# The mean of squares of a norm is read from PSUM by ScalarE, not VectorE

## The chip, the cores and the metric

The kernel runs on one core of a Trainium2 chip. A core has a matrix engine (TensorE, PE in the profile), and beside it VectorE (DVE), ScalarE (ACT), GpSimd (POOL) and SyncE (SP, which here issues the loads and stores). They run side by side, each in its own order of instructions, and wait for each other through semaphores. TensorE writes its results into PSUM, the other engines work on SBUF and PSUM. The metric is the device time of one execution in microseconds, lower is better.

## What is computed

One decoder block on a sequence of 2048 tokens with 1024 channels in fp32. Cut to what matters here:

```python
def rmsnorm(x, g):
    r = lax.rsqrt(jnp.mean(x * x, axis=-1, keepdims=True) + EPS)
    return x * r * g

hn = rmsnorm(h, norm1_g)
u_pool, q, k, v = split(hn @ w_in)
y_pool = pool_mixer(u_pool, pool_w, pool_scale)         # 4 causal window means, each mapped 128x128
o = stick_breaking_attention(q, k, v)                   # 8 heads of 64
mixed = concat([rmsnorm(y_pool, pool_out_g), rmsnorm(o, attn_out_g)])
h = h + mixed @ w_out
up = rmsnorm(h, norm2_g) @ w_up                         # 1024 -> 4096
h = h + jnp.square(jax.nn.relu(up)) @ w_down            # 4096 -> 1024
return rmsnorm(h, final_g)
```

There are five kinds of norm: before the input projection, over the pooled half, over the attention half, before the up projection, and the final one. Each is made once for each block of 512 tokens.

## The kernel before

The 2048 tokens are four blocks of 512; a block lies as 8 chunks of 128 channels (the partitions) by 512 tokens. Products keep fp32 accuracy by splitting both operands: ScalarE makes the high part (L146, `hi`), VectorE the low part as the difference (L147), and `products` (L178 to L180) issues three matmuls for each pair of chunks. A rounded operand and its rest are written in one tile, so `hl<-raw` by ACT is the high part of a weight granule and `hl<-raw,hl` by DVE its low part; `h<-nt` and `h<-nt,h` are the same for the normed activation, `sa`, `hw`, `ad`, `wd` for the operands of the feed-forward. Weight granules are loaded five ahead (`weights`, `load_raw`).

The stages in order of time: the input projection of the four blocks (`pd` tiles) with the pooling groups (`pp`) between; attention (`pz` scores, a running product on VectorE as `pc`, `pta` transposes, `po` values), cut into small pieces that are put between the matmuls of the projection; the output projection with the residual; the up projection (`pX`, `pY`, `pZ`, L1082) and the down projection (`pb`, L1249 and L1422), both by a scheme that needs seven block products instead of eight and so has sums on VectorE (L919 to L922, L1021 to L1048).

A norm goes through the engines in a fixed chain. ScalarE and VectorE sum the squares of the chunks (`ss`). TensorE multiplies by a column of 1/n, which gives the mean of squares `pm` with the tokens on partitions, 128 x 4 (L205). VectorE reads `pm` out of PSUM, adds epsilon and writes `m` into the SBUF tile `v` (L213). GpSimd makes the root in `v`: a first guess by integer arithmetic (L214) and three Newton steps of four instructions (L221 to L224), then casts the root to its high part and takes the low part (L241 and L242 as `yr`, L821 and L822 as `yrlast` for the last block, L1290 and L1291 for the final norm). TensorE then spreads the root over 128 partitions with 8 small matmuls (L231, `pr`), the first of which needs the cast. ScalarE copies `pr` out (`r`, L251), and VectorE multiplies the chunks (`nt<-xt,gains,r`, L263). Of the 21 roots that a run makes, 18 are made by GpSimd; the first norm of all and the last two roots of the end are made on VectorE instead.

The norm before the up projection of the last block is special: its root is made in two halves of a tile `yrlast` (`root_last`), called at step 1 of the loop in `up`, and its two spreads are written at steps 6 and 10 of that loop.

No order of instructions is written down for the machine: the framework's scheduler takes the program as written, with its own estimate of how long every instruction takes, and sets one order on each engine. The instructions of `inv_rms` have a raised priority. So an instruction that moves between engines also changes the order around it. There is a second branch for inputs that need more of the attention; it is not executed.

Of the kernel before, what the change touches and what calls it, by code (L numbers as in the profile page):

```python
# [12 lines left out]
AF = mybir.ActivationFunctionType  # L13
ALU = mybir.AluOpType
# [18 lines left out]
EPS = 1e-6  # L33
# [13 lines left out]
def hymba_block(ctx: ExitStack, tc: tile.TileContext, xT, gains, w_in, pool_w, w_out, w_up, w_down, out):  # L47
    nc = tc.nc
# [160 lines left out]
    def inv_root(pm, eng):  # L209

        v, w = vp.tile([P, 3 * TB], F32, tag="v", name="v"), pm.shape[-1]
        m, y, t = v[:, 0:w], v[:, TB:TB + w], v[:, 2 * TB:2 * TB + w]
        nc.vector.tensor_scalar(m, pm, 1.0, EPS, op0=ALU.mult, op1=ALU.add)  # L213
        eng.tensor_scalar(y.bitcast(I32), m.bitcast(I32), -0.5, float(0x5F3759DF), op0=ALU.mult, op1=ALU.add)  # L214
        for _ in range(3):
            if eng is nc.vector:
                eng.scalar_tensor_tensor(t, y, -0.5, y, op0=ALU.mult, op1=ALU.mult)
                eng.tensor_tensor(t, t, m, ALU.mult)
                eng.scalar_tensor_tensor(y, t, 1.5, y, op0=ALU.add, op1=ALU.mult)
            else:  # L220
                eng.tensor_tensor(t, y, y, ALU.mult)  # L221
                eng.tensor_tensor(t, t, m, ALU.mult)
                eng.tensor_scalar(t, t, -0.5, 1.5, op0=ALU.mult, op1=ALU.add)
                eng.tensor_tensor(y, y, t, ALU.mult)  # L224
        return y
# [9 lines left out]
    def inv_rms(ss, n, r=None, eng=None, early=False):  # L235

        eng = eng or nc.gpsimd
        with tc.high_priority():
            y = inv_root(mean_squares([ss], n, psz if early else None, "pz" if early else "px"), eng)
            yr = tmp.tile([P, 2, TB], F32R, tag="yr", name="yr")  # L240
            eng.tensor_copy(yr[:, 0], y)  # L241
            eng.tensor_tensor(yr[:, 1], y, yr[:, 0].bitcast(F32), ALU.subtract)  # L242
            where, tag = (psx, "px") if eng is nc.vector else (psz, "pz") if early else (pst, "pt")
            pr = where.tile([P, T], F32, tag=tag, name="pr")
            marks["pr"] = spread(pr, yr)
            if eng is not nc.vector:
                g = state["tick"]
                gates.extend([(g + 10, marks["pm"]), (g + 14, marks["pr"])])
            if r is None:
                r = tmp.tile([P, T], F32, tag="r", name="r", bufs=2)  # L250
            nc.scalar.activation(r, pr, AF.Copy)  # L251
            return r
# [566 lines left out]
    def root_last(i, ss, where=None, tag="px"):  # L819
        y = inv_root(mean_squares([ss], D, where, tag), nc.gpsimd)  # L820
        nc.gpsimd.tensor_copy(yrlast[:, i, 0], y)  # L821
        nc.gpsimd.tensor_tensor(yrlast[:, i, 1], y, yrlast[:, i, 0].bitcast(F32), ALU.subtract)  # L822
# [275 lines left out]
    def down(pools):  # L1098
# [187 lines left out]
        def final_root(j, acc, ss, r):  # L1286

            y = inv_root(mean_squares([ss], D, psb, f"b{free}"), nc.gpsimd)
            yr = tmp_.tile([P, 2, TB], F32R, tag="yr", name="yr", bufs=3)
            nc.gpsimd.tensor_copy(yr[:, 0], y)  # L1290
            nc.gpsimd.tensor_tensor(yr[:, 1], y, yr[:, 0].bitcast(F32), ALU.subtract)  # L1291
            roots.append((j, acc, r, yr))
# [321 lines left out]
```

## Time and profile before

| what | value |
|---|---|
| median of 3 runs | 1913.86 us (1912.65 to 1914.35) |
| profiled execution, its own time | 1917.71 us |
| its span | 1915.9 us |
| granted TensorE clock, mean | 0.995 |
| TensorE busy | 1891.8 us, 99% |
| VectorE busy | 1424.4 us, 74% |
| ScalarE busy | 1006.7 us, 53% |
| GpSimd busy | 177.7 us, 9% |

The profile is one execution; its own time is 3.85 us above the median of the runs. Start times are counted from the span's start. In a timeline row stand start, length, engine, line, operation, output and inputs with their shapes, how many, and in brackets the idle time before the row with what ended it. In a waits row stand the total of the waits, how many, and the longest.

### The profile page before, as it was taken

Reading aid. Unit: us, or ns where it says so; the run is one execution under the profiler, and the core shown is the slowest. Engines: PE = TensorE matmul, PEld = TensorE weight load, DVE = VectorE, ACT = ScalarE, POOL = GpSimd, SP = SyncE. Lnnn points to the kernel's source line nnn. Section 1 sums busy time; section 2 is a strip of 40 time slices with the busy share of each in tenths; the row PEclk is TensorE's granted clock in tenths of the full one; section 3 lists DMA queues with packets and bytes.
Section 4 is the critical chain, followed back from the end, with each engine's and each line's share of the span. In section 5 each row is a group of like instructions: output and inputs, shape, how many; then the busy total and the mean of one; then the engine's idle time right before and its main releaser. Section 6 shows DMA issues by size and latency. Waiting matters only on the chain.

```text
span 1915.9 us, 26510 instructions
## 1 busy us (share of the span) xinstructions
PE 1891.8 (99%) x8995; PEld 1577.8 (82%) x8995; DVE 1424.4 (74%) x2128; ACT 1006.7 (53%) x1598; POOL 177.7 (9%) x399
## 2 busy tenths in 40 slices
PE   9999999999999999999999999999999999999997
PEld 7888888888888888788888888887888888888886
DVE  6887799667866886776787877786655547888874
ACT  5565566555554465455566555454333345656643
POOL 0211113101211030000000000000010010020120
PEclk9999999999999999999999999999999999999998
DMA  6686596787887867776777677778998889899862
GB/s 213 204 270 201 191 295 221 244 312 264 283 321 295 282 239 252 261 254 227 273 285 269 233 258 262 243 266 310 379 358 308 282 253 314 291 297 334 295 209 91
DMA packets 206034, 509.68 MB, mean 266 GB/s; under 512 B 24256, under 2 KB 30400, under 8 KB 202048
## 3 DMA queue, kind: packets, MB, share of 16 engines
q1 hardware_dynamic: 201136, 499.24, 75.1%
q0 software_dynamic: 4608, 8.39, 2.4%
q8 instruction: 73, 1.20, 0.3%
q14 instruction: 73, 0.60, 0.1%
q10 hardware_dynamic: 144, 0.26, 0.0%
HBM read 335.82 MB, written 171.97 MB: 265 GB/s over the span
## 4 chain that ended last, share of the span: by engine, by line
PE 89%; DMA 4%; DVE 4%; issue 1%; ACT 1%; POOL 0%; SPq 0%; DVEq 0%; ACTq 0%
PE pY L1082 16%; PE pb L1422 16%; PE pb L1249 12%; PE pZ L1082 8%; PE pd L178 8%; PE pd L180 8%; PE pd L179 8%; PE pX L1082 4%; PE po L675 2%; PE pta L664 1%; DMA xt<-in_xT_dram 1%; PE pr L231 1%; DMA t<-in_w_down_dram 1%; PE pm L205 1%; PE pz L617 1%; DMA wr<-in_w_down_dram 1%
## 5 line engine op out<-in xcount | busy, mean ns | idle before, releaser
L1082 PE MATMUL pY<-sa,hw 128*128 128x512 f32 x1536 | 365.7, 389 | 0.7 <-ACT u L1015 0.7
L1422 PE MATMUL pb<-ad,wd 128*128 128x512 f32 x1488 | 340.9, 390 | 1.3 <-ACT ad L146 1.2
L1082 PEld LDWEIGHTS pY<-sa,hw 128*128 128x128 f32 x1536 | 288.1, 188 | 60.9 <-ACT u L1015 1.1
L1422 PEld LDWEIGHTS pb<-ad,wd 128*128 128x128 f32 x1488 | 278.5, 188 | 60.0 <-ACT ad L146 1.6
L178 PE MATMUL pd<-h,hl 128*128 128x512 f32 x752 | 299.8, 399 | 0.7 <-DVE qkr L424 0.7
L180 PE MATMUL pd<-h,hl 128*128 128x512 f32 x752 | 296.9, 395 | 0.0
L179 PE MATMUL pd<-h,hl 128*128 128x512 f32 x752 | 296.7, 395 | 0.0
L147 DVE TENSOR_TENSOR ad<-ar,ad 128x1024 fp32r<-128x1024 f32 x148 | 179.8, 1221 | 70.2 <-ACT ad L146 70.0
L1249 PE MATMUL pb<-ad,wd 128*128 128x512 f32 x1008 | 229.2, 389 | 0.5 <-DVE ad L147 0.5
L1249 PEld LDWEIGHTS pb<-ad,wd 128*128 128x128 f32 x1008 | 189.0, 188 | 40.4 <-DVE ad L147 1.2
L146 ACT ACTIVATE ad<-ar 128x1024 fp32r<-128x1024 f32 x148 | 155.6, 1053 | 116.8 <-issue 47.6
L1082 PE MATMUL pZ<-sa,hw 128*128 128x512 f32 x768 | 186.7, 390 | 1.5 <-DVE a L1032 1.5
L1082 PEld LDWEIGHTS pZ<-sa,hw 128*128 128x128 f32 x768 | 143.9, 188 | 32.2 <-DVE a L1032 2.4
L178 PEld LDWEIGHTS pd<-h,hl 128*128 128x128 f32 x752 | 142.1, 189 | 28.2 <-DVE qkr L424 1.0
L180 PEld LDWEIGHTS pd<-h,hl 128*128 128x128 f32 x752 | 141.8, 189 | 28.0
L179 PEld LDWEIGHTS pd<-h,hl 128*128 128x128 f32 x752 | 142.0, 189 | 27.1
L146 ACT ACTIVATE hl<-raw 128x512 fp32r<-128x512 f32 x168 | 104.0, 631 | 111.2 <-PE pd L180 70.7
L147 DVE TENSOR_TENSOR hl<-raw,hl 128x512 fp32r<-128x512 f32 x168 | 114.1, 685 | 53.6 <-ACT hl L146 50.0
L147 DVE TENSOR_TENSOR hw<-rt,hw 128x512 fp32r<-128x512 f32 x128 | 86.8, 686 | 51.4 <-ACT hw L146 51.3
L1009 ACT ACTIVATE a<-a 128x512 f32<-128x512 f32 x96 | 59.5, 630 | 86.8 <-DVE a L1048 41.4
L146 ACT ACTIVATE wd<-wr 128x1024 fp32r<-128x1024 f32 x40 | 42.4, 1060 | 112.4 <-PE pb L1422 94.1
L1082 PE MATMUL pX<-sa,hw 128*128 128x512 f32 x384 | 93.1, 389 | 0.0
(219 smaller groups left out, 2652.2 us busy)
## 6 DMA issues: line engine op xcount, KB each, us to landing
ar<-sd SPq DMA_DIRECT2D x100, 512.0 KB, 5.4
wr<-in_w_down_dram SPq DMA_DIRECT2D x64, 512.0 KB, 5.4
rb<-in_w_up_dram SPq DMA_DIRECT2D x30, 1024.0 KB, 6.4
sd<-a SPq DMA_DIRECT2D x112, 256.0 KB, 4.0
raw<-in_w_in_dram SPq DMA_DIRECT2D x50, 512.0 KB, 4.5
ar<-sdi SPq DMA_DIRECT2D x48, 512.0 KB, 5.7
sd<-s SPq DMA_DIRECT2D x88, 256.0 KB, 4.0
sdi<-hr SPq DMA_DIRECT2D x72, 256.0 KB, 4.4
```

The lines of the kernel that those rows point to most:

```text
L146: nc.scalar.activation(hi, src, AF.Copy)
L147: return nc.vector.tensor_tensor(lo, src, hi.bitcast(F32), ALU.subtract)
L178: nc.tensor.matmul(ps, hl[:, 0, c], hi, start=(k == 0), stop=False)
L179: nc.tensor.matmul(ps, hl[:, 0, c], lo, start=False, stop=False)
L180: mm = nc.tensor.matmul(ps, hl[:, 1, c], hi, start=False, stop=(k == n - 1))
L205: marks["pm"] = nc.tensor.matmul(pm[:, c:c + 1], ss[:, c * P:(c + 1) * P], inv[n], start=(i == 0), stop=(i == len(parts) - 1))
L231: mm = nc.tensor.matmul(pr[:, b * P:(b + 1) * P], yr[:, x, b:b + 1].to_broadcast([P, P]), identr, start=(b == 0 and x == 0), stop=(b == TB ...
L675: nc.tensor.matmul(po[:, p * 256 + to:p * 256 + to + hi - lo], vw[:, 2 * p + v], at[:, x, lo:hi], start=(p == 0 and n == 0 and x == 0), sk ...
L1009: nc.scalar.activation(t, src, AF.Relu)
L1082: nc.tensor.matmul(t, w[:, wx, c], a[:, ax, c % 2], start=first and c == 0 and x == 0, stop=last and c == G - 1 and x == 2, skip_group_che ...
L1249: nc.tensor.matmul(b, t[:, wx, 2 * (kk % 2) + c, i * P:(i + 1) * P], a[:, ax, c], start=p in ("P1", "P5", "P2") and kk == 0 and c == 0 and ...
L1422: nc.tensor.matmul(ps[q, n], block(t, wx, c, n), left_[q][:, ax, c], start=(n_ in ("P1", "P3") and kk == 0 and c == 0 and x == 0), stop=(n ...
```

## The change

In `inv_root`, the read of `pm` goes to ScalarE where the root is made on GpSimd, as a copy with epsilon as its bias. The three roots that VectorE makes keep their read.

```diff
         v, w = vp.tile([P, 3 * TB], F32, tag="v", name="v"), pm.shape[-1]
         m, y, t = v[:, 0:w], v[:, TB:TB + w], v[:, 2 * TB:2 * TB + w]
-        nc.vector.tensor_scalar(m, pm, 1.0, EPS, op0=ALU.mult, op1=ALU.add)
+        if eng is nc.vector:
+            nc.vector.tensor_scalar(m, pm, 1.0, EPS, op0=ALU.mult, op1=ALU.add)
+        else:
+            nc.scalar.activation(m, pm, AF.Copy, bias=EPS)
         eng.tensor_scalar(y.bitcast(I32), m.bitcast(I32), -0.5, float(0x5F3759DF), op0=ALU.mult, op1=ALU.add)
```

The lines behind it stand three further down in the changed file (L1082 is L1085, L231 is L234). The number of instructions is the same but for 18 that change the engine; the scheduler sets another order. At the places below, the numbers behind names tell apart the tiles of one name.

TensorE at the up projection, before, at the two spreads of the last block's root (`pr_8313` for the first half of `yrlast`, `pr_8410` for the second):

```order
L231 MATMUL pr_8313<-identr_103,yrlast_146 128x128 x8
L1082 MATMUL pX_8353<-sa_7869,hw_8269 128x512 x2
L1082 MATMUL pY_8129<-sa_8121,hw_8144 128x512 x6
L1082 MATMUL pY_8129<-sa_8126,hw_8144 128x512 x6
...
L1082 MATMUL pZ_8397<-sa_7908,hw_8323 128x512 x6
L231 MATMUL pr_8410<-identr_103,yrlast_146 128x128 x8
L1082 MATMUL pY_8272<-sa_8121,hw_8346 128x512 x6
```

The same place after:

```order
L234 MATMUL pr_8313<-identr_103,yrlast_146 128x128 x8
L1085 MATMUL pX_8353<-sa_7869,hw_8269 128x512 x2
L234 MATMUL pr_8410<-identr_103,yrlast_146 128x128
L1085 MATMUL pY_8129<-sa_8121,hw_8144 128x512 x6
L1085 MATMUL pY_8129<-sa_8126,hw_8144 128x512 x6
...
L1085 MATMUL pZ_8397<-sa_7908,hw_8323 128x512 x6
L234 MATMUL pr_8410<-identr_103,yrlast_146 128x128 x7
```

The first of the eight matmuls of the second spread has moved ahead of 70 matmuls, to the place behind two of `pX_8353`; the other seven stay where all eight were. ScalarE's read of the mean for this second half stands right behind the high part of `sa_8154`; VectorE's order there is the same, less the read.

VectorE before, late in the input projection, with the read for the pooled half's norm (`v_5682<-pm_5677`):

```order
L147 TENSOR_TENSOR at_5512<-pta_5507,at_5512 128x512
L147 TENSOR_TENSOR hl_5640<-raw_5536,hl_5640 128x512
L213 TENSOR_SCALAR v_5682<-pm_5677 128x4
L147 TENSOR_TENSOR at_5585<-pta_5580,at_5585 128x512
L629 SCALAR_TENSOR_TENSOR pc_5612<-sh_5618 128x256 x2
```

ScalarE after, at the same place:

```order
L146 ACTIVATE at_5512<-pta_5507 128x512
L146 ACTIVATE hl_5640<-raw_5536 128x512
L216 ACTIVATE v_5682<-pm_5677 128x4
L146 ACTIVATE at_5585<-pta_5580 128x512
L626 ACTIVATE sh_5618<-pz_5611 128x512
```

The read stands behind the split of the same weight granule `hl_5640` on either engine: behind its low part before, behind its high part after. On TensorE the spread of this root, `pr_5700`, which stood behind the five score matmuls of `pz_5719` and five of `pd_5742`, stands after the change between the second and the third of those score matmuls.

TensorE in the tail, before, at the first two spreads of the final norm (`ad` and `wd` with the numbers of one step of the down projection):

```order
L1422 MATMUL pb_17161<-ad_17151,wd_17148 128x512 x6
L231 MATMUL pr_17249<-identr_103,yr_17212 128x128
L1422 MATMUL pb_17168<-ad_17151,wd_17148 128x512
L231 MATMUL pr_17249<-identr_103,yr_17212 128x128 x7
...
L1422 MATMUL pb_17168<-ad_17246,wd_17243 128x512 x6
L1422 MATMUL pb_17175<-ad_17246,wd_17243 128x512 x6
L1422 MATMUL pb_17154<-ad_17306,wd_17303 128x512
L231 MATMUL pr_17366<-identr_103,yr_17329 128x128 x8
```

After:

```order
L1425 MATMUL pb_17161<-ad_17151,wd_17148 128x512 x6
L1425 MATMUL pb_17168<-ad_17151,wd_17148 128x512 x6
L1425 MATMUL pb_17175<-ad_17151,wd_17148 128x512
L234 MATMUL pr_17249<-identr_103,yr_17212 128x128 x8
...
L1425 MATMUL pb_17168<-ad_17246,wd_17243 128x512 x6
L234 MATMUL pr_17366<-identr_103,yr_17329 128x128 x8
L1425 MATMUL pb_17175<-ad_17246,wd_17243 128x512 x6
```

The first spread comes seven matmuls later, the second seven earlier. ScalarE reads the second mean behind the high part of `ad_17423`; VectorE read it behind eight scalings of finished chunks (L1299) and ahead of the low parts of `wd_17303` and `ad_17423`.

In the first stage, the spread of the second block's first norm, `pr_858`, comes seven matmuls earlier on TensorE. Behind it, before, ten matmuls of `pd_1386` (which takes that block's chunks) were followed by the 24 of `pd_1509` (which takes the first block's) and then by the rest of `pd_1386`; after, nineteen of `pd_1386` come first. VectorE multiplies the first three chunks of that block ahead of one more low part and one more pooling sum.

## The prediction

> **What bounds the kernel now.** I read the page's busy shares first, then the chain of work that ended last, then the table of TensorE's waits.
>
> ```profile
> PE 1891.8 (99%) x8995; PEld 1577.8 (82%) x8995; DVE 1424.4 (74%) x2128; ACT 1006.7 (53%) x1598; POOL 177.7 (9%) x399
> PE 89%; DMA 4%; DVE 4%; issue 1%; ACT 1%; POOL 0%; SPq 0%; DVEq 0%; ACTq 0%
> PE pr L231 <- DVE pc L629: 2.5, 1, 2.5
> PE pZ L1082 <- DVE a L1032: 1.5, 2, 1.2
> PE pr L231 <- POOL yr L1290: 0.9, 1, 0.9
> PE pd L178 <- DVE qkr L424: 0.7, 1, 0.7
> ```
>
> TensorE is the bound: 1891.8 us busy, and 89% of the last chain. VectorE and ScalarE have spare time, so an instruction taken from one and put on the other is worth nothing by itself. What counts is whether TensorE waits somewhere. In the waits (total, times, longest) two are a norm's spread `pr`, held by the root: 2.5 us and 0.9 us (POOL's root ends last in both, as its rows below show). So I look at each norm: when the mean is read, when the root is cast, and when TensorE reaches the spread.
>
> **The moved read itself.** It leaves VectorE at 0.155 us and arrives on ScalarE at a price the trace does not show.
>
> ```profile
> L213 DVE TENSOR_SCALAR v<-pm x19: 136/155/164, 31.8 to 1864.5; 128x4 f32<-128x4 f32 x19
> L146 ACT ACTIVATE at<-pta 128x512 fp32r<-128x512 f32 x56 | 33.4, 599 | 11.6 <-PE pta L664 9.5 <-PE po L675 1.4
> L146 ACT ACTIVATE at<-pta 128x384 fp32r<-128x384 f32 x8 | 4.0, 495 | 3.7 <-PE pta L664 3.6
> ```
>
> The nearest rows are ScalarE copies out of PSUM. 512 elements take 0.599 us and 384 take 0.495, so the line through both puts 4 elements at 0.495 − 380 × 0.104/128 = 0.19 us. The lower bound is VectorE's 0.14, the upper the 0.495 of the nearest row. I take 0.19, an estimate; 18 × 0.19 = 3.4 us on an engine 53% busy, which I cost at nothing: idle ScalarE time hides it. VectorE gains 18 × 0.155 = 2.8 us it does not need. What changes the time is the new order: TensorE's spreads are placed elsewhere. I go through the places where the rows leave less than 1 us of room or the spread moved; elsewhere I book nothing.
>
> **The last-block norm (703 to 717 us), the largest term.** Start and length are the first two columns, but for the first row: a step of POOL, shortest/median/longest ns.
>
> ```profile
> L214 POOL TENSOR_SCALAR v<-v x18: 192/193/6379, 63.9 to 1864.8; 128x4 int32<-128x4 int32 x18
> 703.32 0.95 PE L205 MATMUL pm<-inv,sslast 128*128 128x1 f32 x8
> 703.95 1.05 ACT L146 ACTIVATE sa<-sr 128x1024 fp32r<-128x1024 f32 x1
> 706.37 0.15 DVE L213 TENSOR_SCALAR v<-pm 128x4 f32<-128x4 f32 x1
> 706.62 6.38 POOL L214 TENSOR_SCALAR v<-v 128x4 int32<-128x4 int32 x1 [27.09 <-DVE v L213]
> 716.76 0.19 POOL L821 CAST yrlast<-v 128x4 fp32r<-128x4 f32 x1
> 712.88 2.88 PE L1082 MATMUL pY<-sa,hw 128*128 128x512 f32 x12
> 728.75 1.00 PE L231 MATMUL pr<-identr,yrlast 128*128 128x128 f32 x8
> 705.17:712.95 7.78, 7.78 (x40) 6.58 (x39) 7.78 (x13) 5.91 (x10) 6.33 (x1) 1.00 0.64 226
> ```
>
> The last row is busy time in that stretch (length, PE, PEld, DVE, ACT, POOL, clock, DMA share, GB/s): VectorE is busy for all of it, and POOL's first step of the root, 0.193 us in its usual rows, sits there for 6.38 us. VectorE's work there is mostly operations on two SBUF tensors. POOL gets on when VectorE pauses at 713, and the cast that TensorE needs ends at 716.95. Before, that costs nothing: the spread is at 728.75. After, its first matmul stands right behind two `pX` matmuls and ahead of the twelve of `pY`, where TensorE is at 712.88. The read moves up: pm ends at 704.27, ScalarE's `sa` at 705.00, so the mean is there at about 705.2 instead of 706.52. But POOL's step then falls on the same VectorE run, whose order is unchanged but for the read. So the cast still ends at about 716.9, and TensorE stands still for 716.9 − 712.9 = 4.0 us. Bounds: 0 (the cast is ready) and 4.2.
>
> A wait also slows the clock afterwards, as the next place shows: I add 1.7 us, bounds 0 and 3.4 (two slices). **Term: +5.7.**
>
> **The stall at 457 us.**
>
> ```profile
> 447.98 1.02 PE L205 MATMUL pm<-inv,ss 128*128 128x1 f32 x8
> 452.76 0.64 ACT L146 ACTIVATE hl<-raw 128x512 fp32r<-128x512 f32 x1 [3.21 <-DMA raw<-in_w_in_dram]
> 454.03 0.15 DVE L213 TENSOR_SCALAR v<-pm 128x4 f32<-128x4 f32 x1
> 460.08 0.51 POOL L241 CAST yr<-v 128x4 fp32r<-128x4 f32 x1
> 457.73 0.39 PE L179 MATMUL pd<-h,hl 128*128 128x512 f32 x1
> 460.64 0.33 PE L231 MATMUL pr<-identr,yr 128*128 128x128 f32 x1 [2.52 <-DVE pc L629]
> 462.19:465.60 3.41, 3.41 (x10) 2.63 (x9) 2.68 (x4) 1.20 (x3) 0.00 (x0) 0.50 0.96 325
> ```
>
> The mean is ready at 449, but VectorE first makes the low part of `hl_5640`, whose load arrived at 452.7. On ScalarE the read stands behind the high part of that same `hl_5640`, so the load still holds it: it comes at 453.5, some 0.5 us earlier. The cast comes 0.2 to 0.6 earlier (VectorE's low part still holds POOL to about 454.1). Yet the spread stands six matmuls, 6 × 0.23 = 1.4 us, earlier. So the wait grows from 2.5 to about 3.5: **+1.0**, bounds +0.5 and +2.7 (a second slow slice). The windows row is the price of a gap: for 3.41 us behind it the granted clock is 0.50, which loses half of it, 1.7 us; that is paid already and stays.
>
> The Trainium skill, TensorE: Matmul & The Clock Gate, Part 1, warns of idle gaps over about 3.4 us; this trace disagrees, since 2.52 us of idling sufficed. By that rule the sum without the slow slices that I add would be 2.6 us less, 1922.
>
> **The first stage (60 to 85 us).**
>
> ```profile
> 60.53 0.62 ACT L146 ACTIVATE hl<-raw 128x512 fp32r<-128x512 f32 x1
> 63.61 0.15 DVE L213 TENSOR_SCALAR v<-pm 128x4 f32<-128x4 f32 x1
> 70.09 0.19 POOL L241 CAST yr<-v 128x4 fp32r<-128x4 f32 x1
> 71.43 0.22 PE L231 MATMUL pr<-identr,yr 128*128 128x128 f32 x1
> 72.70 0.60 ACT L251 ACTIVATE r<-pr 128x512 f32<-128x512 f32 x1 [1.79 <-PE pr L231]
> 73.38 2.07 DVE L263 SCALAR_TENSOR_TENSOR nt<-xt,gains,r 128x512 f32<-128x512 f32 x3
> 81.05 0.50 PE L178 MATMUL pd<-h,hl 128*128 128x512 f32 x1 [0.70 <-DVE qkr L424]
> ```
>
> ScalarE is free at 61.15, so the read comes 2 us earlier, but POOL's first step waits for a gap in VectorE's run near 63.6: the cast gains 0 to 0.5 us. The spread stands seven matmuls (1.6 us) earlier, so it waits about 0.2, and `r` and the normed chunks come some 1.4 us earlier. The order spends this and more: it runs nineteen matmuls of `pd_1386` in a row where before it ran ten and then the 24 of `pd_1509`, which need no new chunk. TensorE is at the fourth chunk at 80.1; VectorE, at 0.6 to 0.7 us a step from 72.0 in its new order, has that chunk's low half at 80.9 (wait 0.5), the sixth's at 82.7 (0.5), the seventh's source at 83.4, copied at 84.1 (1.2), and frees the bank of `pd_1509` by `qkr` at 85.3 (1.0). That is 0.2 + 0.5 + 0.5 + 1.2 + 1.0 = 3.4 against the 1.0 of before (0.70, and 0.27 just ahead of it): **+2.4**, bounds −1 (all of before's waits go) and +5 (the attention pieces, now packed closer behind, wait twice more for 1.3 us).
>
> **The tail (1820 to 1838 us).**
>
> ```profile
> 1820.44 0.33 PE L231 MATMUL pr<-identr,yr 128*128 128x128 f32 x1 [0.87 <-POOL yr L1290]
> 1824.21 0.95 PE L205 MATMUL pm<-inv,ss 128*128 128x1 f32 x8
> 1825.38 1.04 ACT L146 ACTIVATE ad<-ar 128x1024 fp32r<-128x1024 f32 x1
> 1827.77 0.15 DVE L213 TENSOR_SCALAR v<-pm 128x4 f32<-128x4 f32 x1
> 1828.01 2.23 POOL L214 TENSOR_SCALAR v<-v 128x4 int32<-128x4 int32 x1 [7.33 <-DVE v L213]
> 1835.53 0.19 POOL L1290 CAST yr<-v 128x4 fp32r<-128x4 f32 x1
> 1836.26 1.00 PE L231 MATMUL pr<-identr,yr 128*128 128x128 f32 x8
> ```
>
> The first spread moves seven matmuls later (1.6 us), so its 0.87 us wait goes: −0.9. The second moves seven earlier, on a TensorE that is 0.9 earlier: it is reached at 1836.26 − 0.9 − 1.6 = 1833.8. Its mean is read on ScalarE behind `ad`, at 1826.5, but VectorE's two-tensor run (the eight scaled chunks, `wd`, `ad`) still holds POOL to about 1830.5; the cast stays near 1836.0. Wait 2.2, with half a slow slice (0.9): **+2.2** for both, bounds −0.9 and +3.0.
>
> **Given back later:** TensorE's two waits at `pZ` (1.5 us) fall behind the new wait at 713, on work that VectorE and the loads do meanwhile. I take half, **−0.7**, bounds 0 and −1.5.
>
> Sum: 5.7 + 1.0 + 2.4 + 2.2 − 0.7 = +10.6 us. The profiled run took 1917.71 us (span 1915.9), 3.85 over the median of 1913.86; the sum goes onto the median: 1924.5.
>
> **The rivals.**
> *POOL gets in between VectorE's instructions.* If a waiting POOL step ran at the end of the VectorE instruction in progress, the 14 steps would need about 10 boundaries before 712.95 and 4 × 0.28 us behind: cast at 714.3, wait 1.4, no slow slice (0.87 us brought none), and no second wait in the tail. Sum 1.4 + 1.0 + 2.4 − 0.9 − 0.2 = +3.7, 1917.6. Against it speaks the 6.38 us row, where some twelve boundaries passed. The Trainium skill, SBUF — State Buffer, section on the two separate sides, says the shared port pair is locked "for the whole instruction" only, which is this rival; the trace disagrees.
> *The gains of an earlier root win (faster).* Place: the stall at 457. If the load of `hl_5640` came at 449.6 or earlier, 3.1 us before now, the mean would be read at 450.4 and the cast be there when TensorE is: 2.5 + 1.7 = −4.2, 1909.7. It decides only if the wait at 713 is under 0.4. Against it: nothing in the change moves that load.
> *The change does nothing of note.* Casts come as the new order expects, the first stage sheds its 1.0 us, and 457's +1.0 is all that is left: 1913 to 1915.
> *Each gap costs whole slow slices.* Two at 713, one more at 457 and in the tail, the first stage at +5: 4.0 + 3.4 + 2.7 + 5 + 3.0 = +18, 1932.
>
> **How the numbers follow.** Forecast 0.60 (1918.5 to 1930); POOL between instructions 0.13, half of it under the bound; nothing of note 0.07; faster 0.06; whole slices 0.14. A change of under 0.2%, 3.8 us, can't be told from none here: faster 0.06, same 0.07 + 0.06 = 0.13, slower 0.81. The range leaves out the faster rival, and the ends of the others: 1914.5 to 1932.
>
> **What would show it.** A wait of about 4 us at the single matmul of the second `yrlast` spread, with a POOL row of some 6 us ahead of it and a clock slice near 0.50 behind; 3.5 us at the 457 spread; four short waits in the 80s; no wait at the first tail spread and about 2 at the second. I am wrong if POOL's root is not held at 705, if VectorE's run there breaks up, or if ScalarE's read costs microseconds.

## The result, and the profile after

The changed kernel takes 1923.61 us (median of 7 runs, 1918.35 to 1929.42), the kernel before 1913.48 us (7 runs, 1912.15 to 1914.35). The ratio is 1.0058 with a 95% interval of 1.0042 to 1.0075: the change costs 10 us. The profiled run took 1929.42 us, its span is 1927.6 us; it is the slowest of the seven, 5.8 us above their median, so single profiles show the places of the cost better than its size. Two later measurements of the same kernel gave 1.0065 and 1.0071, so the cost is 10 to 13 us.

The busy shares and the chain of the changed kernel:

```profile
PE 1896.9 (98%) x8995; PEld 1579.8 (82%) x8995; DVE 1420.8 (74%) x2110; ACT 1009.6 (52%) x1616; POOL 180.3 (9%) x399
PE 82%; DVE 7%; DMA 7%; issue 1%; ACT 1%; POOL 1%; SPq 0%; DVEq 0%; ACTq 0%
```

VectorE lost 18 instructions and 3.6 us of busy time, ScalarE gained 18 and 2.9 us, and neither matters. The span grew by 11.7 us, TensorE's busy time by 5.1 (matmuls at half clock are longer), the rest is idling. The chain says the same: VectorE and the loads have a larger part in it. TensorE's waits, with total, times and longest:

```profile
PE pr L234 <- POOL yrlast L824: 2.6, 1, 2.6
PE pm L205 <- DVE ss L189: 2.5, 1, 2.5
PE pZ L1085 <- DVE a L1035: 1.9, 1, 1.9
PE pr L234 <- POOL yr L1293: 1.5, 1, 1.5
PE ptv L444 <- DVE vf L439: 0.9, 1, 0.9
PE pd L178 <- DVE qkr L427: 0.7, 1, 0.7
PE pd L178 <- ACT h L146: 0.6, 1, 0.6
PE pd L179 <- DVE h L147: 0.5, 1, 0.5
PE po L678 <- ACT qk L146: 0.4, 1, 0.4
```

The first row is the new wait at the second `yrlast` spread. The second is the stall that stood at 457 us: in this profile it is ahead of the mean, not behind it. The fourth is the second spread of the tail. The last five are new or lie at another place, and all in the first stage.

The moved read itself costs what a small copy out of PSUM costs (shortest, median and longest in ns):

```profile
L216 ACT ACTIVATE v<-pm x18: 153/174/206, 58.8 to 1875.9; 128x4 f32<-128x4 f32 x18
```

**Where the time is.** The table gives the time that TensorE lost in a stretch, in us: the distance from one matmul's start to the next, less the usual distance for that shape, summed. It holds the waits and the half-clock matmuls behind them. The last three columns are experiments (below); where there are several profiles of one kernel, each is given, in the order of the runs.

| us from the start | before | changed, 3 profiles | second spread put back, 2 | early read put back | last block alone, 2 |
|---|---|---|---|---|---|
| 0 to 25 | 5.9 | 3.2, 5.1, 3.0 | 3.3, 4.0 | 4.3 | 3.5, 5.3 |
| 75 to 125 | 2.4 | 8.0, 10.3, 8.0 | 6.4, 6.5 | 2.4 | 2.6, 2.4 |
| 425 to 475 | 6.1 | 5.5, 7.3, 6.4 | 5.6, 6.4 | 7.2 | 6.2, 4.2 |
| 675 to 725 | 0.1 | 5.7, 1.0, 6.9 | 0.9, 0.6 | 3.9 | 1.8, 1.8 |
| 775 to 825 | 2.1 | 2.6, 0.6, 0.2 | 0.3, 0.5 | 1.8 | 1.4, 1.1 |
| 1000 to 1050 | 0.0 | 1.0, 0.9, 0.3 | 0.6, 1.5 | 0.8 | 0.0, 0.2 |
| 1800 to 1850 | 1.3 | 3.7, 1.8, 1.8 | 1.8, 3.5 | 3.7 | 1.3, 1.3 |
| whole span | 31.8 | 43.2, 41.0, 39.3 | 31.4, 35.4 | 36.0 | 29.1, 27.8 |

The first row is the start of the kernel, which the change does not touch: it differs by 2 to 3 us from execution to execution. Three places carry the cost: the first stage, the last block's spread, and the tail.

**The first stage.** TensorE's waits in the timeline between 77 and 83 us, and where the attention pieces stand:

```profile
78.11 0.50 PE L179 MATMUL pd<-h,hl 128*128 128x512 f32 x1 [0.53 <-DVE h L147]
81.24 0.51 PE L178 MATMUL pd<-h,hl 128*128 128x512 f32 x1 [0.59 <-ACT h L146]
82.44 0.50 PE L178 MATMUL pd<-h,hl 128*128 128x512 f32 x1 [0.70 <-DVE qkr L427]
...
112.53 0.35 PE L678 MATMUL po<-at,vw 128*128 128x256 f32 x1 [0.44 <-ACT qk L146]
113.07 0.56 PE L678 MATMUL po<-at,vw 128*128 128x256 f32 x3 [0.19 <-DVE at L147]
114.57 0.66 PE L444 MATMUL ptv<-ident,vf 128*128 128x128 f32 x4 [0.94 <-DVE vf L439]
```

With a shorter one at 79.4 us, the waits around 80 us lose 2.7 us, those at the attention pieces 2.1. Behind the latter, the matmuls run at half clock for one slice, though only 1.50 us (3.41 − 1.91) of the slice ahead of it were idle. In the windows (length; busy time of PE, PEld, DVE, ACT, POOL; granted clock; DMA share; GB/s) the slice in which the pieces wait, and the next:

```profile
112.16:115.57 3.41, 1.91 (x11) 1.52 (x12) 3.38 (x7) 2.32 (x5) 0.00 (x0) 1.00 0.86 269
115.57:118.99 3.42, 3.42 (x10) 2.64 (x9) 3.42 (x8) 0.63 (x1) 1.10 (x1) 0.50 0.95 325
```

**The last block's norm.** The changed kernel at the second `yrlast` spread:

```profile
706.23 0.16 ACT L216 ACTIVATE v<-pm 128x4 f32<-128x4 f32 x1
706.47 6.79 POOL L217 TENSOR_SCALAR v<-v 128x4 int32<-128x4 int32 x1 [25.87 <-ACT v L216]
717.11 0.19 POOL L824 CAST yrlast<-v 128x4 fp32r<-128x4 f32 x1
714.11 0.67 PE L1085 MATMUL pX<-sa,hw 128*128 128x512 f32 x2
717.35 0.47 PE L234 MATMUL pr<-identr,yrlast 128*128 128x128 f32 x1 [2.56 <-POOL yrlast L824]
717.62 5.43 PE L1085 MATMUL pY<-sa,hw 128*128 128x512 f32 x12
```

The read is early, GpSimd's first step is held for 6.79 us all the same, TensorE waits 2.56 us, and the twelve `pY` matmuls behind it take 5.43 us where they took 2.88 before.

**The tail.**

```profile
1830.01 1.00 PE L234 MATMUL pr<-identr,yr 128*128 128x128 f32 x8
1834.16 0.15 ACT L216 ACTIVATE v<-pm 128x4 f32<-128x4 f32 x1
1836.56 2.84 POOL L226 TENSOR_SCALAR v<-v 128x4 f32<-128x4 f32 x1
1844.17 1.28 PE L234 MATMUL pr<-identr,yr 128*128 128x128 f32 x8 [1.50 <-POOL yr L1293]
```

The first spread no longer waits; the second waits 1.50 us, with half clock behind it. In the other two profiles of the changed kernel the second waits 1.25 us and keeps its clock.

### The profile page after: what moved, and what is told of

Read it like the earlier page. It is cut to its first block, busy times and chain, and to the rows that moved or that the text cites. A ratio compares the mean times of both kernels' runs of the same rounds, so it can differ in the third digit from the quotient of the medians.

```text
span 1927.6 us, 26508 instructions
## 1 busy us (share of the span) xinstructions
PE 1896.9 (98%) x8995; PEld 1579.8 (82%) x8995; DVE 1420.8 (74%) x2110; ACT 1009.6 (52%) x1616; POOL 180.3 (9%) x399
## 4 chain that ended last, share of the span: by engine, by line
PE 82%; DVE 7%; DMA 7%; issue 1%; ACT 1%; POOL 1%; SPq 0%; DVEq 0%; ACTq 0%
PE pb L1425 16%; PE pY L1085 14%; PE pb L1252 12%; PE pd L178 7%; PE pd L179 7%; PE pd L180 7%; PE pZ L1085 7%; PE pX L1085 3%; PE po L678 2%; DMA sr<-su 1%; PE pta L667 1%; DMA t<-in_w_down_dram 1%; PE pr L234 1%; PE pz L621 1%; PE pz L620 1%
## 5 line engine op out<-in xcount | busy, mean ns | idle before, releaser
L1085 PE MATMUL pY<-sa,hw 128*128 128x512 f32 x1536 | 368.7, 391 | 1.5 <-ACT u L1018 0.9
L1085 PEld LDWEIGHTS pY<-sa,hw 128*128 128x128 f32 x1536 | 289.4, 189 | 63.5 <-ACT u L1018 2.5
L1085 PE MATMUL pZ<-sa,hw 128*128 128x512 f32 x768 | 186.4, 389 | 1.9 <-DVE a L1035 1.9
L1085 PEld LDWEIGHTS pZ<-sa,hw 128*128 128x128 f32 x768 | 143.9, 188 | 32.3 <-DVE a L1035 2.3
L1085 PE MATMUL pX<-sa,hw 128*128 128x512 f32 x384 | 93.2, 390 | 0.0
```

The costliest lines, as they stand in the source:

```text
L1085: nc.tensor.matmul(t, w[:, wx, c], a[:, ax, c % 2], start=first and c == 0 and x == 0, stop=last and c == G - 1 and x == 2, skip_group_che ...
```

## The experiments

The theory: what costs time is TensorE's new order, which places spreads ahead of roots that come no sooner. The first rival: the read is dear on ScalarE, so that the cost goes by the number of reads.

### One group of reads at a time

The 18 reads fall into three groups whose new orders lie at different places: 13 ahead of the up projection, 2 of the last block's norm, 3 of the final norm. Each kernel takes the change for one of them (`site` is handed in by the callers):

```diff
-    def inv_root(pm, eng):
+    def inv_root(pm, eng, site="front"):
...
-        if eng is nc.vector:
+        if eng is nc.vector or site not in ("last0", "last1"):
```

The last block alone (two reads):

> Only the two reads of the last block's norm (root_last) are on ScalarE; the other 16 stay on VectorE. TensorE's order differs from before only from the second yrlast spread on. Theory (TensorE's new order makes it wait): the profile of the changed kernel lost 5.6 us at that spread (2.7 waiting, 2.9 at half clock) and 1.3 us more at pZ and pY behind it, so +5 to +7 us over before, about 1919.5. Rival (the read is dear on ScalarE): the 10.1 us go by the number of reads, 2 of 18, +1.1 us, 1914.6.

1914.81 us against 1913.62, ratio 1.0009 (0.9999 to 1.0019), runs from 1912.81 to 1921.28. The theory's sum, +5 to +7, was missed; the median of +1.2 is the rival's +1.1. But the profile shows the theory's wait at the second spread, only shorter and with no half clock behind it. POOL and TensorE in this kernel:

```profile
702.41 0.77 POOL L217 TENSOR_SCALAR v<-v 128x4 int32<-128x4 int32 x1 [25.98 <-ACT v L216]
703.26 0.52 POOL L224 TENSOR_TENSOR v<-v 128x4 f32<-128x4 f32 x1
711.47 0.19 POOL L824 CAST yrlast<-v 128x4 fp32r<-128x4 f32 x1
711.71 0.33 PE L234 MATMUL pr<-identr,yrlast 128*128 128x128 f32 x1 [1.45 <-POOL yrlast L824]
```

The first step is not held to the end of VectorE's run here; this step and the next last 0.77 and 0.52 us, about one VectorE instruction each. That is what the prediction's first rival described, and the wait of 1.45 us is the 1.4 that it worked out.

The final norm alone (three reads):

> Only the three reads of the final norm are on ScalarE. Theory: the tail alone, -1.0 at the first spread and +3.6 at the second (1.7 waiting, the rest half clock): +2.5 us, 1916. Rival (dear read, 3 of 18): +1.7. These two are close; what tells them apart is the profile: no wait at the first tail spread, one of 1.5 to 2.5 us at the second.

1914.85 us, ratio 1.0011 (1.0002 to 1.002): +1.2 us. That is less than either sum (+2.5 and +1.7). Its profile has no wait at the first spread and one at the second, as the theory said, but of 1.25 us, under the 1.5 to 2.5 expected, and no half clock behind it:

```profile
1816.10 1.00 PE L234 MATMUL pr<-identr,yr 128*128 128x128 f32 x8
1830.01 1.28 PE L234 MATMUL pr<-identr,yr 128*128 128x128 f32 x8 [1.25 <-POOL yr L1293]
```

The 13 norms ahead of the up projection:

> Only the 13 reads of the norms ahead of the up projection are on ScalarE. Theory: four short waits between 77 and 82 us (2.7 in all against 1.0 before), waits at the attention pieces near 112 us (2.1, and up to 1.7 of half clock behind them), 450 us about even: +3.5 to +5, about 1917.7. Rival (dear read, 13 of 18): +7.3, 1920.8.

1918.87 us, ratio 1.0031 (1.0021 to 1.0042): +5.3 us, just above the theory's +3.5 to +5 and below the rival's +7.3. Per read that is 0.4 us, against 0.6 for the two of the last block, so the medians of these kernels do not refute the rival of the dear read. The next two kernels do.

### All reads on ScalarE, one spread put back

```diff
-                spread(pr, yrlast[:, i])
+                with tc.issue_after(mm.ins) if i else nullcontext():
+                    spread(pr, yrlast[:, i])
```

`mm` is the last matmul of the step. TensorE's order in the up projection is then that of before, and all 18 reads stay on ScalarE.

> All 18 reads on ScalarE, but the second yrlast spread is held behind the matmuls of its own step, which gives TensorE the order of before in the up projection and leaves the rest as changed. Theory: the 5.6 us and the 1.3 us behind them go, 1923.6 - 6 = about 1917.5, with no wait at the second spread although its cast is as late as before. Rival (dear read): no difference from the changed kernel, 1923.6.

1917.98 us against 1913.62, ratio 1.0032 (1.002 to 1.0043). The second spread waits for nothing in its profile. The changed kernel stood at 1923.61 in another session: with all 18 reads left on ScalarE, about 5.6 us are gone (5.2 in one session, below). The dear read can't be what these cost; it is the place of the spread.

### All reads on ScalarE but one

The second block's first norm keeps its read on VectorE; everything else is as changed (`act` is a new argument of `inv_root`, true if not given).

```diff
-        if eng is nc.vector:
+        if eng is nc.vector or not act:
...
-            y = inv_root(mean_squares([ss], n, psz if early else None, "pz" if early else "px"), eng)
+            y = inv_root(mean_squares([ss], n, psz if early else None, "pz" if early else "px"), eng, not early)
```

> As changed, but the second block's first norm (the spread at 71 us before) keeps its read on VectorE; TensorE's order differs from the changed kernel only between 65 and 160 us, where it is that of before. Theory: the waits at 77 to 82 us and at the attention pieces near 112 us, with the half clock behind them, are due to this one read: 3.5 to 5 us less than the changed kernel, about 1918. Rival (many small costs of the 13 reads): no more than 1 us less.

Beside it, the changed kernel again:

> The changed kernel once more, on the same terms as the kernels that hold one part of the change each. Those were, as medians, +1.2 (last block's norm), +1.2 (final norm) and +5.3 (norms ahead of the up projection) over 1913.6. If the parts add up: 1921.3. If the last block's wait is dearer behind a changed front (in the first profile it lost 5.6 us, alone 1.6): 1923 to 1926. The second profile tells whether the wait at the second yrlast spread and the half-clock slices behind the waits are the same in every execution.

1918.61 us with the early read put back, 1925.66 us as changed, before 1912.54: ratios 1.0029 (1.0017 to 1.004) and 1.0065 (1.0048 to 1.0081). One read out of 18 is worth 7 us, where 3.5 to 5 were expected. The table's column shows why: the first stage lost 2.4 us as before, not 8 to 10, a difference of 5.6 to 7.9. Its waits around 80 us are back to one of 0.97, and the attention pieces' 2.1 us and the half clock are gone. Read and order go back together here, so the order is shown as the cause for the last block only, and argued for the first stage from the rows.

### Do the parts add up?

They did not: 5.3 + 1.2 + 1.2 = 7.7 us against 10 to 13. So four corners were measured side by side.

> One of four corners measured side by side: front and tail changed or not, the second yrlast spread early or not (before, the last block's read alone, the early spread undone, all changed). Theory: the early spread costs the same in both surroundings, one wait of 0.6 to 2.6 us and, when enough of it falls into one slice of the clock's grid, 1.7 us of half clock behind it: about 3 us each, so this kernel stands 3 us over the one with the early spread undone. Rival: it is dear only behind the changed front (5.6 to 7.7 us here, 1.2 alone, as the first medians had it).

> The early spread undone, the rest as changed. Theory: +6 to +8 over before (the front's 4 to 7, the tail's 1). Rival: +4.4, as in its first run.

> The last block's read alone. Theory: +2 to +4 over before, and the same distance as between the changed kernel and the one with the early spread undone. Rival: +1.2 again.

| | early spread undone | early spread |
|---|---|---|
| front and tail as before | 1913.96 (before) | 1915.38, ratio 1.0011 (1.0002 to 1.0019) |
| front and tail as changed | 1921.25, ratio 1.0043 (1.003 to 1.0055) | 1926.46, ratio 1.0071 (1.0058 to 1.0084) |

The early spread costs 1.4 us alone and 5.2 us behind the changed front. My expectation of the same 3 us in both is not borne out, and the rival stands, though with 5 and 6 runs in the lower row not by much: by means the two prices are 2.1 and 5.3 us, and their difference of 3.1 has a standard error of 1.3. Part of the 5.2 us need not lie at the spread: in both profiles with the second spread put back the first stage has no half-clock slice and loses 6.4 and 6.5 us, in all three of the changed kernel it has one or two and loses 8.0 to 10.3.

The profiles show one thing that differs at the spread itself. POOL's first step and TensorE's wait in the changed kernel at this corner:

```profile
708.82 6.98 POOL L217 TENSOR_SCALAR v<-v 128x4 int32<-128x4 int32 x1 [25.96 <-ACT v L216]
719.78 0.47 PE L234 MATMUL pr<-identr,yrlast 128*128 128x128 f32 x1 [3.99 <-POOL yrlast L824]
```

And in the second of its three profiles:

```profile
712.79 0.56 POOL L217 TENSOR_SCALAR v<-v 128x4 int32<-128x4 int32 x1 [25.00 <-ACT v L216]
721.72 0.33 PE L234 MATMUL pr<-identr,yrlast 128*128 128x128 f32 x1 [0.62 <-POOL yrlast L824]
```

GpSimd's first step was held until VectorE's run was over, or had one instruction left, in two of three profiles of the changed kernel (waits 2.56 and 3.99 us, half clock behind both) and in none of the three with the early spread and the front's early read on VectorE (0.77, 0.56 and 0.77 us; waits of 1.45, 1.45 and 1.90, half clock behind the last). So the same order has two prices, by whether GpSimd is held. But this does not show that the changed front brings the hold. Over all kernels, the step was held in two of the six profiles with the first stage's new order (0.44 to 1.70 us in the other four) and in two of the five with the old one (6.38 us both before and with the final norm alone). Nor does the hold carry the time by itself: the execution without it took 1927.19 us, the held ones 1929.42 and 1925.88. Why the early spread is dearer behind the changed front stays open.

### What holds GpSimd, and what slows the clock

Three kernels measured these two by themselves. VectorE runs sums of two SBUF tiles back to back, GpSimd's steps on 128x4 are released at a moment that is shifted from run to run. The first:

```python
for i in range(n):
    with tc.issue_after(last.ins):
        last = nc.vector.tensor_tensor(o, xa, second, ALU.add)
nc.gpsimd.tensor_scalar(y.bitcast(I32), m.bitcast(I32), -0.5, float(0x5F3759DF), op0=ALU.mult, op1=ALU.add)
nc.gpsimd.tensor_tensor(t, y, y, ALU.mult)
```

> Nothing of the block is computed: the output is filled from one tile. First 28 runs of 14 VectorE sums of two SBUF tiles, then 10 of an SBUF and a PSUM tile; in each, four GpSimd steps on 128x4 start at another moment, released by ScalarE. Rule A (GpSimd gets in at the end of the VectorE instruction in progress, as in the profile with the last block's read alone): each step lasts 0.5 to 0.7 us in the first runs. Rule B (it is held until VectorE pauses, as in the profile of before): the first step lasts 5 to 8 us. Both: 0.2 us in the runs with PSUM. Then 28 bursts of 40 matmuls of 128x512, with gaps on TensorE from about 1 to 5 us between. If the idle share of a 3.413 us slice decides, half-clock slices begin behind gaps near 1.9 us, not behind each; if a whole idle slice is needed, only behind gaps over 3.4 us.

With the sums writing one tile, they start 0.727 us apart, though each lasts 0.69. GpSimd's first step then took 0.19 to 0.74 us in all 28 runs: it got in at the end of the sum in progress, which is rule A of the expectation. With an input from PSUM it took 0.19 us in all 10. Then the sums read other tiles and write four tiles in turn:

```diff
-        last = nc.vector.tensor_tensor(o, xa, second, ALU.add)
+        last = nc.vector.tensor_tensor(os[i % 4][:, 0:w], big[:, 0:w], second[:, 0:w], ALU.add)
```

> Nothing of the block is computed. As in the first runs of the kernel that measured the hold alone, but VectorE's sums write four tiles in turn, so that they follow each other at 0.60 us as in the block, not at 0.73 with a pause between: 28 runs of 14 sums of 128x512, 28 with sums of 128x512 and 128x1024 mixed, 20 in which VectorE itself releases GpSimd, 6 with a PSUM input. If the pause between the sums is what lets GpSimd in: its steps now last until the run ends, 3 to 8 us, in some or all of the runs with two SBUF tiles. If a step gets in at the end of any sum: 0.5 to 1.2 us, as before. With PSUM 0.2 us in both.

Now they start 0.602 us apart and last 0.68, so each starts before the one ahead has ended, as in the block. Two successive runs, and one with PSUM, on POOL:

```profile
13.88 7.75 POOL L94 TENSOR_SCALAR v<-v 128x4 int32<-128x4 int32 x1 [7.37 <-ACT v L84]
...
23.42 0.49 POOL L94 TENSOR_SCALAR v<-v 128x4 int32<-128x4 int32 x1 [0.95 <-ACT v L84]
24.00 0.52 POOL L95 TENSOR_TENSOR v<-v 128x4 f32<-128x4 f32 x1
...
704.89 0.19 POOL L94 TENSOR_SCALAR v<-v 128x4 int32<-128x4 int32 x1 [0.89 <-ACT v L84]
```

Both rules hold, in turn: every second run held the first step until VectorE's last sum ended (7 to 8 us), the other runs let each step in at the next end of a sum. The moment of arrival made no difference, nor did VectorE as the releaser. The last kernel varied the counts:

> Nothing of the block is computed. In the dense runs GpSimd's first step was held to the end of every second run, whenever it arrived; each run there had an odd number of VectorE instructions, counted with the one that gates it. Here: 16 runs with an even number, 12 with an odd one, 16 in an irregular mix, 8 with three GpSimd steps instead of four. If the parity of VectorE's instructions decides, the first 16 runs are all alike, the next 12 alternate, and the mix follows its parities. If a toggle that each run flips decides, all alternate, whatever the counts. If the moment of arrival decides, neither. Then 48 gaps on TensorE between about 0.9 and 2.2 us: a half-clock slice follows where more than about 1.5 us of one 3.413 us slice are idle, and not where a gap of up to 2.2 us is cut in two by the grid.

With an even number of VectorE instructions in a run, none of the first 16 was held; with an odd one, they alternated. In the irregular part a held run was never followed by another. One rule, found afterwards, fits all 52 runs: a step is held if the run before was not held and had an odd number of VectorE instructions. It also fits the 76 runs with two SBUF tiles of the kernel ahead of it, but not the 28 with 0.727 us between the sums (15 instructions each, none held). That excludes both of the expected rules, parity alone and a toggle alone. By this rule, what counts is the state in which the runs ahead left the two engines; what that state is in the hardware stays open. The block also has first steps between the two kinds (1.70, 2.23 us), for which these kernels have no counterpart.

The gaps on TensorE, in the same kernel: a gap in one slice, and the slice behind it, three times.

```profile
805.76:809.17 3.41, 1.64 (x7) 1.05 (x6) 0.00 (x0) 1.62 (x5) 0.00 (x0) 1.00 0.00 0
809.17:812.58 3.41, 3.41 (x16) 2.81 (x15) 0.00 (x0) 0.00 (x0) 0.00 (x0) 1.00 0.02 5
816.00:819.41 3.41, 1.62 (x7) 1.04 (x6) 0.00 (x0) 1.64 (x5) 0.00 (x0) 1.00 0.00 0
819.41:822.82 3.41, 3.41 (x10) 2.63 (x8) 0.00 (x0) 0.00 (x0) 0.00 (x0) 0.50 0.00 0
942.29:945.70 3.41, 1.40 (x7) 1.16 (x7) 0.00 (x0) 1.86 (x5) 0.00 (x0) 1.00 0.00 0
945.70:949.11 3.41, 3.41 (x10) 2.66 (x9) 0.00 (x0) 0.00 (x0) 0.00 (x0) 0.50 0.00 0
```

With 1.77 us of the slice idle the next one keeps its clock (16 matmuls), with 1.79 and 2.01 us it runs at half (10). The expectation had put this at about 1.5. The boundaries of the slices lie on one grid of 3.413 us through an execution, at a place against the kernel's start that differs between executions, so the same wait costs 1.7 us more or nothing, as the grid cuts it: of the twelve gaps of 1.79 to 2.01 us in this kernel the five that lay whole in one slice were followed by half clock, the seven that the grid cut were not, though one of these had 1.86 us in one slice.

In the block the limit is less sharp. Over all profiles of this study but the last 25 us of each, with the idle time taken from the PE column of the windows, of slices at full clock with 0.8 to 1.2 us idle none of 58 was followed by half clock, with 1.2 to 1.8 us 13 of 50, with more 30 of 31. Of the 13, 11 lie in the block, from 1.27 us on, and the two of the gap kernels have 1.79. One slice of the block even had 0.76 us, where the eight matmuls of a mean, one column each, stand (448.7 us in the corner's profile of the changed kernel). So idle time as the profile counts it does not decide alone there; what else does was not measured.

## Why the prediction was right, point by point

1924.5 us was forecast with a range of 1914.5 to 1932, 1923.61 was measured. The direction and the mechanism held. That the total came within 1 us is partly luck: by the lost time, as a mean over the three profiles, the first stage cost 6.4 us where 2.4 were booked, while the last block (4.4 for 5.7), the tail (1.1 for 2.2) and the stall at 457 us (0.3 for 1.0) cost less than booked.

- **The read** was put at 0.19 us and at nothing on the path. It takes 0.153 to 0.206 us (median 0.174), and with the second spread put back the 18 reads stay and 5.6 us go.
- **The last block, +5.7.** The place, the one matmul that waits, the held step and the half clock behind it came as said. Lost time there was 5.7, 1.0 and 6.9 us in three profiles, and 5.2 us between medians of one session (7.7 and 5.6 across sessions). The wait of 4.0 us was met once (3.99), where the hold ended as late as before; in the first profile the hold ended 1.5 us earlier against TensorE, so the wait was 2.56. Both had two half-clock slices behind the wait, where one was booked. The reading that POOL gets on when VectorE pauses at 713 was off by one instruction: POOL's step ended at 713.00, and VectorE went on to 713.57.
- **The rival that GpSimd gets in between VectorE's instructions** had a chance of 0.13 and happens: in one of three profiles of the changed kernel and in all three others that have the early spread. The prediction rejected it on one row of 6.38 us, when the same profile had rows of 0.5 us beside it (0.51 for the cast at 460.08); both kinds occur.
- **The 457 us stall, +1.0.** It came to −0.6, +1.2 and +0.3. The working failed at "the mean is ready at 449". In the changed kernel the mean's own input is late:

```profile
450.83 1.15 ACT L146 ACTIVATE hl<-raw 128x512 fp32r<-128x512 f32 x2 [5.54 <-DMA raw<-in_w_in_dram]
451.49 0.69 DVE L147 TENSOR_TENSOR hl<-raw,hl 128x512 fp32r<-128x512 f32 x1 [2.40 <-ACT hl L146]
452.10 0.69 DVE L189 TENSOR_TENSOR ss<-ss,sq 128x512 f32<-128x512 f32 x1
452.93 1.33 PE L205 MATMUL pm<-inv,ss 128*128 128x1 f32 x8 [2.52 <-DVE ss L189]
```

  The sum of squares stands on VectorE behind the low part of a granule whose load is late, and TensorE waits 2.52 us at the mean. Behind that the root is in time for the spread. So it was in two of the three profiles (2.52 and 2.94 us at the mean); in the third TensorE waits 0.76 us at the mean and 2.41 at the spread, where 3.5 were forecast. The stall moved or was divided and about kept its size: 6.1 us before in this stretch, 5.5 to 7.3 after. The "six matmuls" of the working are eight by the order shown, three of them short: 1.5 us in place of 1.4.
- **The first stage, +2.4, was the term of the wrong size: it cost +5.6 to +7.9.** In the first profile its four waits came at the four instructions named, with 0.69, 0.31, 0.76 and 0.98 us lost where 0.5, 0.5, 1.2 and 1.0 were worked out, 1.8 us more than before. What the term lacked lies behind them: the attention pieces' waits, which stood in the bounds and not in the term, came too (2.1 us), and half-clock slices, of which the working of this place has none (1.4 to 1.6 us each, one or two). That GpSimd's first step would be held until 63.6 us was wrong (it began 0.3 us behind the read and took 0.23 us), without effect: the chunks came 1.5 us earlier, where 1.4 was worked out.
- **The tail, +2.2:** +0.5 to +2.4 in the three profiles, +1.2 alone. The first spread's wait went as said; the second's was 1.50, 1.25 and 1.25 us, not 2.2, since most of GpSimd's steps were let in between.
- **Given back later, −0.7:** in the stretch from 775 us −1.0 as a mean over the three profiles, but +0.7 near 1025 us, where nothing was lost before.
- **The two pages weighed.** Idling of 2.52 us was taken as enough for a half-clock slice; the runs put it lower, at 1.79 us within one slice where nothing but a gap was there, and at 1.3 to 1.5 us in some slices of the block. The Trainium skill, TensorE: Matmul & The Clock Gate, Part 1, which warns of idle gaps over about 3.4 us, disagrees with these rows. A turn for GpSimd at the end of each VectorE instruction was set aside too firmly: rows of 0.5 us show it, rows of 6.8 to 7.8 us show the long hold. The Trainium skill, SBUF — State Buffer, section on the two separate sides, has only the first (the shared pair is locked for one whole instruction); the runs agree with it in part.

The changed kernel's runs spread over 11 us in the first session, those of the kernel before over 2. This was not forecast, and it was no property of the change: in the two later sessions it was 6.5 and 2.7 us against 7.5 and 9.0.

No kernel of this study was faster than the one before.

## What to carry to other kernels

Where a scheduler orders the work, an instruction moved to an idle engine is worth what the new order of the busiest engine is worth, so compare the orders, and ask at each consumer that moved up whether its input also comes earlier. A chain of small GpSimd steps beside VectorE work on two SBUF tiles has two lengths, one step for each VectorE instruction, or next to nothing until VectorE's run ends; plan with the longer. A short TensorE wait has a second price, a slice at half clock (1.7 us), which came here in some slices from 1.3 us of idling and nearly always from 1.8 us of the 3.41: two waits of 1 us in one slice can cost more than one of 1.5.

## What the runs showed of the hardware that was not expected

- Half clock on TensorE does not need one long gap: with over 1.8 us idle within a slice of 3.413 us, 30 of 31 were followed by a slice at 0.50, with 1.2 to 1.8 us, in one wait or several, 13 of 50, with 0.8 to 1.2 none of 58 (and one with 0.76).
- GpSimd's small steps beside dense VectorE sums of two SBUF tiles (0.602 us apart) are either let in at each end of a sum (0.5 us a step) or held up to 8 us, until VectorE's run ends. In the kernels of sums alone, which one it is depends on the history of the two engines, not on the moment of arrival; with 0.727 us between the sums, or one input from PSUM, there was no long hold.
